# A two-layer encoder on one core: splits, gates and near-head transposes put in another order

## The chip, the cores and the metric

The kernel runs on one core of a Trainium2 chip. A core has a matrix engine (TensorE, PE in the profile, with its weight loads shown apart as PEld), VectorE (DVE), ScalarE (ACT), GpSimd (POOL) and a queue for transfers (SP). Each engine takes its own instructions strictly in the order written for it, and waits on semaphores for the others. The metric is device time in microseconds, from the first to the last instruction with a small fixed part around it; lower is better.

## The reference, cut to what matters

Two transformer layers over 1024 tokens of width 1024, with 256 memory tokens. Everything is float32.

```python
for l in range(2):
    h = rmsnorm(x, norm_gain[l])
    mk, mv = split(memn @ w_mem_kv[l])
    if l == 0:
        qa, ka, va, qb, kb, vb, qm, gate = split_cols(h @ w_in_even)
        ya = global_gqa(rope(rms(qa)), rope(rms(ka)), va)      # 8 heads of 64
        yb = window_gqa(qb, kb, vb, sink, rel_bias)            # 8 heads, +-128 tokens
        ym = memory_attn(qm, mk, mv)                           # 4 heads of 128
        y = concat(ya, yb, ym) * silu(gate)
    else:
        qc, kc, vc, qm, gate = split_cols(h @ w_in_odd)
        yc = neighborhood_attn(qc, kc, vc, rpb)                # 16 heads, 8 x 16 window
        ym = memory_attn(qm, mk, mv)
        y = concat(yc, ym) * silu(gate)
    x = x + y @ w_out[l]                                       # y: 1536 wide
return rmsnorm(x, final_gain)
```

## The kernel before

Every number is carried as a high and a low part, so that each product of matrices is three matmuls: high by high, high by low, low by high. A *split* is a copy to the high part on ACT (`copy`) and a subtraction for the low part on VectorE (L126 to L128). Weights are split the same way as they arrive (`w_parts`, L1263: `wraw` is the loaded tile, `wh` the copy on ACT, `wl` the subtraction on VectorE or GpSimd by turns).

The stages, in the order of time: the first projections (to about 143 us), the global and memory heads of layer 0, its window heads (about 500 to 671), output projection 0 (to about 778), the front of layer 1 (its projections, to about 1024), the memory heads of layer 1, its near heads (`near`, about 1130 to 1377), and output projection 1 with the final norm.

**The output projection** (`out_project`, L1297) uses a fast scheme of seven products in place of eight, on sums and differences of quarters of y and w. y is 12 rows of 128; each finished row k is multiplied by its gate and stored to memory as five half-width pieces, where rows 6 to 11 also need differences with row k - 6. The seven operands are called y11, t1, t2, t3, y22, y21 and t4. `y_parts` (L1209) loads the six pieces of one operand and splits them; of t1 and t2 the last three pieces are split later, inside the product (`later`). Each product is 72 matmuls of 512 columns, and PE takes them in the order a11 (with y11), s1 (t1), s2 (t2), s3 (t3), s4 (y22), a12 (y21), a22 (t4). The buffers of y22 are those of y11, and those of y21 are t1's.

**The near heads** run a loop over 128 blocks (16 heads of 8 blocks, L1149). In step n it transposes the probabilities of block n - 4 (`flips`, three transposes or two into a `tr` bank, then `p_parts`: copy `ph` on ACT, subtraction `pl` on VectorE), computes the scores of block n (`scores`: two matmuls; then on VectorE the bias addition with the row minimum, on ACT the exponential, on VectorE the reciprocal, on GpSimd the scaling of `pn`), multiplies block n - 5 by v (`values`), and lets PE do 1930 columns of other work (`fill`: k projections, gates, the first output product). PE keeps the order of the program here; the other engines do not.

**Gates.** `gated_steps` (L469) multiplies a finished row by its gate in two halves on VectorE, then makes the differences on GpSimd and the stores and loads on SP; it is a generator, one step of which is taken in each call of `scores` while `jobs` (splits of k weights) has nothing to do, or by `later_job` (L1935) in the last window heads. `gated` (L500) does the same in one go. `gate(k, tag)` (L1954) loads a gate of layer 1 from memory.

**Who sets the order.** Apart from PE in layer 1, a planner orders each engine's instructions: by priority (the order of the program, moved by the offsets in `AHEAD`) among those which its own simulation of time holds ready. `tc.issue_after(i)` ties what is written inside it: those instructions of the block that are on the engine of i are queued behind i. Instructions on other engines are not held by it. `behind_held` (L1202) ties to the last copy and the last low part of the near or window heads.

Of the kernel before, what the change touches and what calls it, by code (L numbers as in the profile page):

```python
# [64 lines left out]
class Trunk:  # L65
# [403 lines left out]
    def gated_steps(self, sg, y, yd, k):  # L469

        nc = self.nc
        first, second = slice(0, 512), slice(512, T)
        dst = yd[k]
        two = lambda t: t.rearrange("p (a n) -> p a n", a=2)
        nc.vector.tensor_tensor(y[:, second], y[:, second], sg[:, second], op=OP.mult)
        yield
        nc.vector.tensor_tensor(y[:, first], y[:, first], sg[:, first], op=OP.mult)
# [595 lines left out]
    def near(self, made, load_q, load_v, gate, yd, fill):  # L1073
# [12 lines left out]
        def scores(n):  # L1086
# [122 lines left out]
    def y_parts(self, yd, tags, kind, after=None):  # L1209
# [3 lines left out]
        for k, t in enumerate(self.halves(tags, F32R)):  # L1213
# [3 lines left out]
            with self.ahead("y"):  # L1217
# [8 lines left out]
                else:  # L1226
                    with self.behind_held(), self.tc.issue_after(after.ins) if after else nullcontext():
# [69 lines left out]
    def out_project(self, w, sd, yd, res, done, tags, banks, first, begun, last=False):  # L1297
# [26 lines left out]
        def products(y, banks, kind, start, ready=()):  # L1324
            ready = deque(ready)
            y, later = y
            ends.clear()
            for u in range(2):
                for i, bank in enumerate(banks):
                    (h, l), = (ready.popleft(),) if ready else weights(i, kind, (u,))  # L1330
                    for k in range(3):
                        for e, (s, m) in enumerate(((h, 0), (h, 1), (l, 0))):
                            end = nc.tensor.matmul(bank, s[:, k, :], y[3 * u + k][m], start=start and u + k + e == 0,
                                                   stop=u == 1 and k + e == 4, skip_group_check=True)
                    ends[u, i] = end
# [9 lines left out]
        def plus(x, p, op=OP.add):  # L1345
            nc.vector.tensor_tensor(x, x, p, op=op)
# [9 lines left out]
        ends = {}  # L1356
# [27 lines left out]
        y = self.y_parts(yd, tags["y"][3], "t3", after[0])  # L1384
        for i in range(4):
            end = product(y, xb[i], weights(i, "s3"), False)
# [6 lines left out]
        y = self.y_parts(yd, tags["y"][4], "y22", ends[1, 3])  # L1393
        for i in range(4):
            ending = product(y, yb[i], weights(i, "s4"), False)
# [7 lines left out]
        y = self.y_parts(yd, tags["y"][5], "y21", end)  # L1403
# [15 lines left out]
        y = self.y_parts(yd, tags["y"][6], "t4", ending)  # L1419
# [515 lines left out]
    def later_job(self, normal):  # L1935

        if self.later_jobs:
            with self.tc.issue_after(normal.ins):
# [3 lines left out]
    def odd(self, w, kvd, yd, vd, mqd, qd, gd):  # L1942
# [119 lines left out]
        for n in range(8):  # L2062
            h, g = divmod(n, 2)
            if g == 0:
                y = self.st("yb", [128, T])
                if h < 3:
# [10 lines left out]
            if g:  # L2077
                self.gated_rows(gate(8 + h), 8 + h, y, yd)
# [107 lines left out]
```

## Time and profile before

| | us |
|---|---|
| median of 3 runs | 1505.27 (1504.47 to 1507.01) |
| the profiled execution | 1505.1 |
| its span, first to last instruction | 1503.3 |
| TensorE busy | 1473.3 |
| VectorE busy | 1032.9 |
| ScalarE busy | 841.2 |
| GpSimd busy | 636.2 |

A row of a timeline gives the start in us, the duration in us, the engine, the line, the operation, the tiles written and read, how many instructions were merged into the row, and in brackets the idle time of the engine before it with what ended it. "SPq" is the issue of a transfer. A row of the wait lists gives who waited for whom, the total in us, the number of times and the longest. Matmuls overlap one another, so the distance between starts, not the duration, is what one costs.

### The profile page before, as it was taken

Reading aid. Unit: us, or ns where it says so; the run is one execution under the profiler, and the core shown is the slowest. Engines: PE = TensorE matmul, PEld = TensorE weight load, DVE = VectorE, ACT = ScalarE, POOL = GpSimd, SP = SyncE. Lnnn points to the kernel's source line nnn. Section 1 sums busy time; section 2 is a strip of 40 time slices with the busy share of each in tenths; the row PEclk is TensorE's granted clock in tenths of the full one; section 3 lists DMA queues with packets and bytes.
Section 4 is the critical chain, followed back from the end, with each engine's and each line's share of the span. In section 5 each row is a group of like instructions: output and inputs, shape, how many; then the busy total and the mean of one; then the engine's idle time right before and its main releaser. Section 6 shows DMA issues by size and latency. Waiting matters only on the chain.

```text
span 1503.3 us, 25289 instructions
## 1 busy us (share of the span) xinstructions
PE 1473.3 (98%) x8377; PEld 1266.8 (84%) x8377; DVE 1032.9 (69%) x2122; ACT 841.2 (56%) x1855; POOL 636.2 (42%) x762
## 2 busy tenths in 40 slices
PE   9999999999999999998999999999999999999997
PEld 8898888989888788786879877888988888888786
DVE  6786777677676677667577766654447778788744
ACT  7743665655655456554445444444447777777442
POOL 1223668556665655533450000002225556754355
PEclk9999999999999999999999999999999999999999
DMA  8966344433444423388653434558675677688833
GB/s 282 323 157 178 111 121 165 126 125 118 129 126 136 133 89 129 120 272 268 197 174 117 139 135 148 151 157 284 200 262 154 209 231 223 218 285 312 284 111 138
DMA packets 173859, 271.90 MB, mean 181 GB/s; under 512 B 15648, under 2 KB 96800, under 8 KB 172704
## 3 DMA queue, kind: packets, MB, share of 16 engines
q1 hardware_dynamic: 173296, 270.20, 56.0%
q8 instruction: 66, 1.08, 0.3%
q14 instruction: 65, 0.53, 0.1%
q10 hardware_dynamic: 432, 0.09, 0.0%
HBM read 174.28 MB, written 83.89 MB: 172 GB/s over the span
## 4 chain that ended last, share of the span: by engine, by line
PE 78%; DVE 7%; DMA 7%; issue 3%; ACT 2%; POOL 1%; SPq 1%; POOLq 0%; DVEq 0%; ACTq 0%
PE pj L241 15%; PE pj L62 10%; PE x L1585 6%; PE tr L132 5%; PE pv L1055 4%; PE y L1585 4%; PE pv L62 3%; PE pj L1319 3%; PE s L62 3%; PE sa L1319 2%; PE pv L1585 2%; PE tr L62 2%; PE s L1319 2%; PE sa L1022 2%; PE sa L1023 2%
## 5 line engine op out<-in xcount | busy, mean ns | idle before, releaser
L124 ACT ACTIVATE ph<-tr 128x512 fp32r<-128x512 f32 (+2 forms) x336 | 180.9, 540 | 118.3 <-PE tr L132 76.9
L537 DVE TENSOR_TENSOR pl<-tr,ph 128x512 fp32r<-128x512 f32 (+2 forms) x336 | 205.5, 615 | 54.0 <-ACT ph L124 52.9
L241 PE MATMUL pj<-H,wh 128*128 128x512 f32 x704 | 234.6, 413 | 0.5 <-DVE vt L312 0.2
L157 POOL TENSOR_SCALAR wh<-wraw 128x512 fp32r<-128x512 f32 x48 | 34.4, 719 | 268.3 <-PE x L1585 234.9
L124 ACT ACTIVATE wh<-wraw 128x384 fp32r<-128x384 f32 (+1 forms) x163 | 89.1, 553 | 89.9 <-PE pj L1319 12.0
L241 PE MATMUL pj<-H,wl 128*128 128x512 f32 x352 | 139.1, 395 | 0.0
L241 PEld LDWEIGHTS pj<-H,wh 128*128 128x128 f32 x704 | 120.0, 189 | 18.7 <-POOL wh L157 0.6
L62 PE MATMUL pj<-H,wh 128*128 128x512 f32 x384 | 121.5, 397 | 0.0
L1108 POOL TENSOR_SCALAR pn<-pn,st 128x384 f32<-128x384 f32 (+1 forms) x128 | 75.3, 589 | 99.6 <-DVE st L1107 58.0
L132 PE MATMUL tr<-ident,P 128*128 128x128 f32 x752 | 115.7, 273 | 0.9 <-DVE pl L537 0.6
L1267 POOL TENSOR_TENSOR wl<-wraw,wh 128x384 fp32r<-128x384 f32 x56 | 61.9, 1107 | 117.8 <-ACT wh L124 101.1
L132 PEld LDWEIGHTS tr<-ident,P 128*128 128x128 f32 x752 | 88.9, 140 | 9.6 <-DVE pl L537 1.7
L1028 ACT ACTIVATE P<-sa,st 128x1024 f32<-128x1024 f32 x64 | 71.5, 1118 | 41.5 <-DVE st L1027 22.7
L1106 ACT ACTIVATE pn<-pn,st 128x384 f32<-128x384 f32 (+1 forms) x128 | 75.1, 587 | 35.0 <-DVE st L1103 32.6
L62 PE MATMUL s<-k,q 128*128 128x384 f32 (+1 forms) x352 | 86.5, 342 | 0.1
L1030 POOL TENSOR_SCALAR P<-P,st 128x1024 f32<-128x1024 f32 x64 | 73.9, 1158 | 29.0 <-DVE st L1029 26.9
L1027 DVE TENSOR_REDUCE st<-sa 128x1 f32<-128x1024 f32 x64 | 77.6, 1218 | 10.9 <-PE sa L1023 10.5
L241 PEld LDWEIGHTS pj<-H,wl 128*128 128x128 f32 x352 | 66.2, 188 | 15.1
L62 PE MATMUL pj<-H,wl 128*128 128x512 f32 x192 | 75.8, 395 | 0.0
L159 POOL TENSOR_TENSOR wl<-wraw,wh 128x512 fp32r<-128x512 f32 x52 | 68.2, 1315 | 9.5 <-ACT wh L124 6.9
L62 PEld LDWEIGHTS pj<-H,wh 128*128 128x128 f32 x384 | 66.6, 189 | 5.5
L840 PE MATMUL pj<-ah,H 128*128 128x256 f32 x384 | 70.5, 282 | 0.2
(558 smaller groups left out, 4172.3 us busy)
## 6 DMA issues: line engine op xcount, KB each, us to landing
wraw<-w_o SPq DMA_DIRECT2D x52, 256.0 KB, 3.7
y<-yb SPq DMA_DIRECT2D x24, 512.0 KB, 3.6
wraw<-s SPq DMA_DIRECT2D x64, 192.0 KB, 3.4
wraw<-w_e SPq DMA_DIRECT2D x44, 256.0 KB, 3.2
k<-k SPq DMA_DIRECT2D x42, 256.0 KB, 4.8
s<-bias SPq DMA_DIRECT2D x56, 192.0 KB, 2.0
y<-sg SPq DMA_DIRECT2D x20, 512.0 KB, 3.6
wq<-w_o SPq DMA_DIRECT2D x40, 256.0 KB, 3.3
```

The source lines that it names most:

```text
L62: return lambda *a, **k: self.tc.keep_in_program_order(getattr(self.engine, name)(*a, **k))
L124: return self.nc.scalar.activation(out, in_, AF.Copy, scale=scale)
L132: self.turned = self.fence = self.pe.transpose(o, i, self.ident)
L241: self.pe.matmul(a[:, :n], s[:, kt % UNIT, :], m, start=(kt == 0 and i == 0), stop=(kt == KT - 1 and i == 2))
L537: self.low = nc.vector.tensor_tensor(pl[:, :n], tr[:, :n], ph[:, :n], op=OP.subtract)
L1027: nc.vector.tensor_reduce(st[:, 0:1], s, axis=AX.X, op=OP.max, negate=True)
L1028: nc.scalar.activation(pt, s, AF.Exp, bias=st[:, 0:1], accum_out=st[:, 1:2])
L1030: self.normal = nc.gpsimd.tensor_scalar(pt, pt, st[:, 2:3], 0.5, op0=OP.mult, op1=OP.mult)
L1106: nc.scalar.activation(o, o, AF.Exp, bias=st[:, 0:1], scale=-1.0, accum_out=st[:, 2:3])
L1108: normal = nc.gpsimd.tensor_scalar(o, o, st[:, 3:4], 0.5, op0=OP.mult, op1=OP.mult)
L1319: last = nc.tensor.matmul(bank, s[:, k, :], y[3 * u + k][m][:, cols], start=start and u + k + e == 0, stop=u == 1 and k + e == 4, skip_gro ...
L1585: self.last = nc.tensor.matmul(bank, ws[s][:, k, :], b[k][m], start=start and k + i == 0, stop=k == UNIT - 1 and i == 2, skip_group_check= ...
```

## The change

- `y_parts` and `products`: the tie of the splits of t3, y22, y21 and t4 is no longer to a matmul but to two instructions: the last weight copy (`self.high`, ACT) and the last addition of a product (`self.added`, VectorE) written at that point. The later splits of t1 and t2 are tied to the last weight copy too.
- `near`: transposes are made for two blocks, n - 5 and n - 4, in each even step; the multiplication by v is of block n - 6 in place of n - 5, and the loop has one step more.
- `gated_steps`: each multiplication and the differences of rows below 6 come after `gap` empty steps (1 in the window heads, 2 in the near heads), and its instructions on VectorE are tied to the last low part (`self.low`) as well as, on GpSimd, to the last scaling.
- The memory heads of layer 1 load their gate when a head begins and not when it ends, into two buffers by turns (`sg` and `mk`), and the fourth head's gate is done in steps during the near heads.

```diff
-    def gated_steps(self, sg, y, yd, k):
+    def gated_steps(self, sg, y, yd, k, gap=1):
...
+        for _ in range(gap):
+            yield
         nc.vector.tensor_tensor(y[:, second], y[:, second], sg[:, second], op=OP.mult)
-        yield
+        for _ in range(gap):
+            yield
         nc.vector.tensor_tensor(y[:, first], y[:, first], sg[:, first], op=OP.mult)
         if k < 6:
-            yield
+            for _ in range(gap):
+                yield
...
-                with self.tc.issue_after(normal.ins):
+                with self.tc.issue_after(normal.ins), self.tc.issue_after(self.low.ins):
                     while jobs and next(jobs[0], self) is self:
...
-        for n in range(128 + 5):
-            if 4 <= n < 132:
-                parts[n - 4] = flips(n - 4)
-                if n == 131:
+        for n in range(128 + 6):
+            for f in (n - 5, n - 4) if n % 2 == 0 else ():
+                if 0 <= f < 128:
+                    parts[f] = flips(f)
+                if f == 127:
                     self.held = self.copies[-1], self.low
...
-            if n >= 5:
-                values(n - 5)
-                if (n - 5) % 16 == 15:
-                    j = (n - 5) // 16
-                    self.later_jobs.append(self.gated_steps(pair[j]["g"], pair[j]["y"], yd, ROWS.index(j)))
+            if n >= 6:
+                values(n - 6)
+                if (n - 6) % 16 == 15:
+                    j = (n - 6) // 16
+                    self.later_jobs.append(self.gated_steps(pair[j]["g"], pair[j]["y"], yd, ROWS.index(j), 2))
...
-    def behind_held(self):
+    def behind_held(self, more=()):
         with ExitStack() as held:
-            for i in self.held:
+            for i in (*self.held, *more):
...
-                    with self.behind_held(), self.tc.issue_after(after.ins) if after else nullcontext():
+                    with self.behind_held(after):
                         self.split(hi, lo, raw)
...
-        self.copy(hf, raw)
+        self.high = self.copy(hf, raw)
...
                     elif later:
-                        with self.behind_held(), self.ahead("y"):
+                        with self.behind_held((self.high,)), self.ahead("y"):
                             self.split(*later.popleft())
...
-            nc.vector.tensor_tensor(x, x, p, op=op)
+            self.added = nc.vector.tensor_tensor(x, x, p, op=op)
...
+            if i == 1:
+                after = self.high, self.added
-        after = [ends[1, 0]]
...
-        y = self.y_parts(yd, tags["y"][3], "t3", after[0])
+        y = self.y_parts(yd, tags["y"][3], "t3", after)
+        after = self.high, self.added
...
-        y = self.y_parts(yd, tags["y"][4], "y22", ends[1, 3])
+        y = self.y_parts(yd, tags["y"][4], "y22", after)
+        after = self.high, self.added
...
-        y = self.y_parts(yd, tags["y"][5], "y21", end)
+        y = self.y_parts(yd, tags["y"][5], "y21", after)
+        after = self.high, self.added
...
-        y = self.y_parts(yd, tags["y"][6], "t4", ending)
+        y = self.y_parts(yd, tags["y"][6], "t4", after)
...
             if g == 0:
                 y = self.st("yb", [128, T])
+                sg = gate(8 + h, ("sg", "mk")[h % 2])
...
-            if g:
-                self.gated_rows(gate(8 + h), 8 + h, y, yd)
+            if g and h < 3:
+                self.gated_rows(sg, 8 + h, y, yd)
+            elif g:
+                self.later_jobs.append(self.gated_steps(sg, y, yd, ROWS.index(11), 2))
```

More of the change, by code (lines that the diff above doesn't have):

```diff
@@ L1201, in behind_held, with y_parts @@
     @contextmanager
-    def behind_held(self):
+    def behind_held(self, more=()):
         with ExitStack() as held:
-            for i in self.held:
+            for i in (*self.held, *more):
                 held.enter_context(self.tc.issue_after(i.ins))
             yield
-    def y_parts(self, yd, tags, kind, after=None):
+    def y_parts(self, yd, tags, kind, after=()):
         nc = self.nc
@@ L1326, in products @@
             y, later = y
-            ends.clear()
             for u in range(2):
@@ L1332, in products @@
                         for e, (s, m) in enumerate(((h, 0), (h, 1), (l, 0))):
-                            end = nc.tensor.matmul(bank, s[:, k, :], y[3 * u + k][m], start=start and u + k + e == 0,
-                                                   stop=u == 1 and k + e == 4, skip_group_check=True)
-                    ends[u, i] = end
+                            nc.tensor.matmul(bank, s[:, k, :], y[3 * u + k][m], start=start and u + k + e == 0,
+                                             stop=u == 1 and k + e == 4, skip_group_check=True)
                     if u:
@@ L1383, in out_project @@
         sums = []
-        y = self.y_parts(yd, tags["y"][3], "t3", after[0])
+        y = self.y_parts(yd, tags["y"][3], "t3", after)
+        after = self.high, self.added
         for i in range(4):
-            end = product(y, xb[i], weights(i, "s3"), False)
+            product(y, xb[i], weights(i, "s3"), False)
             residual(at(c21, i), 4 + i, 1)
@@ L1391, in out_project @@
                 square(at(c22, i), i)
-        y = self.y_parts(yd, tags["y"][4], "y22", ends[1, 3])
+        y = self.y_parts(yd, tags["y"][4], "y22", after)
+        after = self.high, self.added
         for i in range(4):
-            ending = product(y, yb[i], weights(i, "s4"), False)
+            product(y, yb[i], weights(i, "s4"), False)
             with self.ahead("sink"):
@@ L1937, in later_job @@
         if self.later_jobs:
-            with self.tc.issue_after(normal.ins):
+            with self.tc.issue_after(normal.ins), self.tc.issue_after(self.low.ins):
                 if next(self.later_jobs[0], self) is self:
```

1 line of the change is left out of this document (removed).

## The prediction, made before the result was known

> **What bounds the kernel now.** I read the page first, then the table of stages, then the list of who waited for whom on TensorE, and last the timelines of the few places where TensorE waits.
>
> ```profile
> span 1503.3 us, 25289 instructions
> PE 1473.3 (98%) x8377; PEld 1266.8 (84%) x8377; DVE 1032.9 (69%) x2122; ACT 841.2 (56%) x1855; POOL 636.2 (42%) x762
> ```
> ```profile
> 671.00:706.00 35.00, 31.05 (x129) 23.59 (x128) 23.73 (x34) 16.47 (x32) 11.91 (x10) 1.00 0.89 302
> 1128.00:1137.00 9.00, 7.97 (x39) 5.96 (x38) 6.34 (x19) 5.78 (x15) 5.50 (x7) 1.00 0.50 167
> 1137.00:1377.00 240.00, 236.87 (x1384) 204.25 (x1383) 188.62 (x581) 176.46 (x448) 136.83 (x188) 1.00 0.73 236
> 1402.00:1423.00 21.00, 18.86 (x80) 14.72 (x79) 15.18 (x20) 11.75 (x22) 8.59 (x7) 1.00 0.89 315
> ```
> TensorE (PE) is busy for 98% of the span, at a granted clock of 1.00 in all these stretches, so nothing but removed matmuls or removed waits of PE can shorten the run. The change removes no matmul. What can be won is idle time: 4.0 us of 35 in the first output projection (671 to 706), 1.0 of 9 where the near heads begin (1128), 3.1 of 240 in the near heads, 2.1 of 21 in the second output projection (1402). (Columns: the stretch, its length, then busy time and instructions of PE, its weight loads, VectorE, ScalarE and GpSimd, granted clock, DMA share, GB/s.) Who ended PE's waits, over the whole run (total, times, longest):
>
> ```profile
> PE pv L62 <- DVE pl L537: 2.7, 7, 0.8
> PE pj L1333 <- DVE wl L1267: 2.4, 1, 2.4
> PE pj L1319 <- DVE wl L1267: 1.9, 1, 1.9
> PE tr L1333 <- DVE wl L1267: 1.0, 1, 1.0
> PE tr L62 <- POOL pn L1108: 0.9, 2, 0.7
> PE sa L692 <- DVE st L696: 0.9, 2, 0.5
> PE pj L1333 <- ACT wh L124: 0.4, 1, 0.4
> PE pj L1319 <- ACT wh L124: 0.2, 1, 0.2
> ```
> Each of the eight lies in a stage that the change touches; together they are 10.4 us. A wait costs more than its listed idle time, as one of the seven waits for a low part shows (PE, then VectorE):
>
> ```profile
> 1168.62 0.49 PE L62 MATMUL tr<-ident,pn 128*128 128x128 f32 x3
> 1168.86 0.60 PE L62 MATMUL s<-k,q 128*128 128x384 f32 x2
> 1169.30 0.34 PE L62 MATMUL pv<-ph,v 128*128 128x384 f32 x1
> 1169.91 0.44 PE L62 MATMUL pv<-pl,v 128*128 128x384 f32 x1 [0.28 <-DVE pl L537]
> 1170.19 0.62 PE L62 MATMUL pj<-H,wh 128*128 128x512 f32 x2
> 1171.63 0.34 PE L62 MATMUL pv<-pl,v 128*128 128x384 f32 x1
> 1154.20 0.34 PE L62 MATMUL pv<-ph,v 128*128 128x384 f32 x1
> 1154.55 0.63 PE L62 MATMUL pj<-H,wh 128*128 128x512 f32 x2
> ```
> ```profile
> 1168.72 0.67 DVE L475 TENSOR_TENSOR yb<-yb,sg 128x512 f32<-128x512 f32 x1
> 1169.31 0.55 DVE L537 TENSOR_TENSOR pl<-tr,ph 128x384 fp32r<-128x384 f32 x1
> 1193.68 0.91 DVE L477 TENSOR_TENSOR yb<-yb,mk 128x512 f32<-128x512 f32 x1
> ```
> By starts, the two steps from 1169.30 to 1170.19 take 0.89 us; undisturbed (1154.20 to 1154.55) they take 0.35. So 0.54 is lost where 0.28 is listed: 0.26 more for each wait, which I add below.
>
> **The change, part by part.**
>
> *Splits of y tied to ACT and DVE (both output projections).* A tie only orders instructions of the tying instruction's own engine. The old tie of a later product's splits named a matmul, and a split is a copy on ScalarE (ACT) and a subtraction on VectorE (DVE): it held nothing. The trace agrees (two rows of y splits on ACT, and between them bt):
>
> ```profile
> 674.92 0.63 ACT L124 ACTIVATE q<-q 128x512 fp32r<-128x512 f32 x1 [4.15 <-DMA q<-y]
> 675.58 0.60 ACT L124 ACTIVATE bt<-pv 64x512 f32<-64x512 f32 x1
> 686.04 0.63 ACT L124 ACTIVATE va<-va 128x512 fp32r<-128x512 f32 x1 [5.08 <-DMA va<-y]
> ```
> At 674.92 ACT takes a part of y22, which is first multiplied two products later, and sits 4.15 us before it for the load; again 5.08 us before 686.04. Queued behind it are the copies of the weights that PE wants now (wh), and also bt, the last window block, on which the gate of row 7 hangs. With the tie to the last weight copy and the last addition of the product before, these splits come some 16 us later, when their loads have long landed. What goes: 1.0 + 0.4 + 2.4 us and 3 x 0.26, 4.6 at most. What is late next: the loads, whose engines are at 0.89 here and which are not moved, so that the parts of t1 that land last still set some wait. Nothing to 4.6; I take 3.6, near the upper end, because the wait is for the order and not for the bytes PE needs.
>
> The moved splits (6 copies and 6 subtractions to a product, of 0.63 and about 0.68 us) now lie beside the product ahead of their own. They are 4.1 us of DVE in about 17 us of PE (72 matmuls; 129 take 31.05 us in the stretch from 671), next to some 8 additions and 4 weight subtractions: it fits, but any that slips shows as a wait for wl. I charge 1.0 (0 to 3).
>
> In the second output projection the same splits delay the last gate:
>
> ```profile
> 1382.63 0.59 ACT L124 ACTIVATE bt<-pv 64x512 f32<-64x512 f32 x1
> 1392.09 1.50 DVE L475 TENSOR_TENSOR yb<-yb,mk 128x512 f32<-128x512 f32 x1
> 1409.06 4.14 SPq L1223 DMA_DIRECT2D H<-y  x6
> 1415.68 3.88 ACT L124 ACTIVATE H<-H 128x512 fp32r<-128x512 f32 x6
> ```
> The order is bt, the gate's multiplication, the row's stores, the load of t2's last part, and behind it in SP's queue the six loads of t3 (1409.06), whose copies (1415.68) stand ahead of the weights for which PE waits 1.9 and 0.2 us in the list (L1319). With y22's and y21's splits gone from the front, bt and the gate come some 5 us earlier and the chain with them. 1.9 + 0.2 + 2 x 0.26 = 2.6 at most; I take 2.0, since the DMA share is 0.89 here as well.
>
> *Gates tied to low parts, with gaps.* In the near loop one gate multiplication or the gate's split stands directly ahead of the pl that PE waits for in all six waits inside the loop (1168.72 and 1193.68 are two); the seventh is at the end of the loop. Tied behind the low part just traced, and with two calls between the steps, a multiplication comes right after both low parts of a pair, and two iterations pass before the next. 2.7 x 6/7 + 6 x 0.26 = 3.9, and I take it all: what covers the 0.67 to 0.91 us of the multiplication is two iterations, some 3.7 us (240 us for 129 of them); behind it in VectorE's queue stands a bias addition whose block is transposed three iterations later. Where that cover is gone, each of the 14 costs what it costs today. The longer gate chain (10 calls for 7) ends, with its stores and its load on SP and its three GpSimd subtractions, some 5 us later; its buffers are wanted again two pairs later, 30 us. In the window heads the same tie moves a multiplication of that size from before the bias additions (0.9 listed, 1.4 with restarts): 0.6, between 0 and 1.4.
>
> *Transposes of two blocks in one run.* It saves no PE time of its own: three transposes take 0.24 us (1168.62 to 1168.86), and the two 384-wide matmuls after them 0.44 in place of 2 x 0.175, so 0.33, 0.11 each; eight in one run take the same:
>
> ```profile
> 152.28 1.03 PE L132 MATMUL tr<-ident,P 128*128 128x128 f32 x8
> 153.07 0.71 PE L241 MATMUL pj<-H,wh 128*128 128x512 f32 x2
> 153.61 0.39 PE L241 MATMUL pj<-H,wl 128*128 128x512 f32 x1
> ```
> (0.79, and 0.54 after it in place of 2 x 0.24: 0.85, 0.11 each.) What it gives is time: the second block of a pair is used two iterations after its transposes and no longer one, the first still after one. The instructions of VectorE and ACT that meet there, in the near stage:
>
> ```profile
> L1103 DVE CUSTOM_DVE_ANT_0 pn<-s,bm 128x384 f32<-128x384 f32 x92 | 50.8, 552 | 19.1 <-PE s L62 9.6 <-PE pv L62 3.2 <-POOL pn L1108 2.4
> L360 DVE TENSOR_TENSOR k<-pj,k 64x512 fp32r<-64x512 f32 x26 | 17.8, 686 | 1.8 <-ACT k L124 1.4
> L124 ACT ACTIVATE ph<-tr 128x384 fp32r<-128x384 f32 x96 | 46.9, 489 | 18.4 <-PE tr L62 16.7 <-PE s L62 0.3
> ```
> The 26 k evictions that can sit ahead of a low part then hurt half as often: 0.5 (0 to 1.5; their waits are too short to be listed). At the loop's end the last block's parts are used right after their transposes, with no filler left: a copy and a subtraction (0.49 and 0.55) less the matmuls between, so +0.5 lost (0 to 1.0).
>
> *Two gate buffers; the fourth memory gate as later steps.*
>
> ```profile
> 1129.44 1.23 DVE L509 TENSOR_TENSOR yb<-yb,sg 128x1024 f32<-128x1024 f32 x1 [3.19 <-DMA sg<-g]
> ```
> The multiplication holds DVE for 3.19 us for its gate's load, the first near blocks' bias additions wait behind it, and PE finds its first pn late (0.9 listed, in two waits). With the load a head earlier and this gate in steps, 0.9 + 2 x 0.15 goes; I take 1.1. The other three memory gates win nothing, as none of PE's listed waits is theirs; on SP the four loads only go ahead of k's copies by some 0.5 us of issue each.
>
> One contention speaks against it all:
>
> ```profile
> L475 DVE TENSOR_TENSOR yb<-yb,mk x4: 891/914/1501, 1199.8 to 1392.1; 128x512 f32<-128x512 f32 x4
> ```
> The multiplication that took 0.67 us at 1168.72 takes up to 1.50 here: something holds it. The Trainium skill (SBUF — State Buffer, "SBUF: two separate sides") says that a VectorE instruction with two SBUF inputs and a GpSimd one that reads SBUF exclude each other for a whole instruction; by that rule the trace agrees, and the moved splits, which have two SBUF inputs, would meet GpSimd's weight subtractions anew. By the rows alone I keep the 1.0 charged above; with the rule taken hard the sum would be that of the second rival.
>
> **Sum.** 3.6 + 2.0 + 3.9 + 0.6 + 0.5 + 1.1 = 11.7 won, 1.0 + 0.5 = 1.5 lost, 10.2 net: 1505.1 us of the profiled execution (span 1503.3 and 1.8 around it) gives 1494.9. The median shown, 1505.27, is 0.2 above it, so 1495. All upper ends and no charge give 4.6 + 2.6 + 3.9 + 1.4 + 1.5 + 1.2 = 15.2, 1490.
>
> **The rivals.** First, *the loads end last.* For it: a DMA share of 0.89 in both output stretches, and loads that keep their order. Against it: ACT's 4.15 and 5.08 us are for parts wanted much later. Then the output projections give a third, 1.9 in place of 5.6: 1498.6, and with the upper charges (3 and 1.0) 1501.1.
>
> Second, *splits and weight subtractions hold each other.* A held one takes 1.50 for 0.68, 0.82 more. Of the 24 splits of y22 and y21 in two layers, one in five reaching PE costs 5 x (0.82 + 0.26) = 5.4: 1500.3.
>
> Third, *the change does not do what it says*: the planner, which orders by its own estimate of time, puts other early work in the places freed, and the waits only change names. Then only the 1.1 of the fourth memory gate is left, 1504.
>
> Fourth, the other side: *pairs make the first block late.* From the end of its transposes (1168.95) to its low part's use at 1171.63 are 2.68 us, 2.1 without the 0.54 lost between; copy and subtraction take 0.49 and 0.55, hand-overs some 0.3, so 0.8 is spare. One VectorE operation of 0.68 ahead of pl fits; in a pair the second block's copy and subtraction and a bias addition of 0.55 come into the same stretch, and if a second one goes ahead, PE waits about 0.4 + 0.26. From 16 of 64 pairs on (16 x 0.66 = 10.6) the gain is gone; at every second pair, 32 x 0.66 = 21, it is 1516. Against it: 20% of DVE's time is free there, and the spare time of the first block is what it is today.
>
> **How the numbers follow.** A measurement of this kernel tells 0.2% (3 us) from no change. Forecast (1490 to 1499): 0.48. First and second rival (1499 to 1502): 0.22. Third, between 1502.3 and 1508.3: 0.12. Fourth, or a new order that costs as much: 0.18. Faster 0.70, same 0.12, slower 0.18. The range leaves out a tenth at each side: 1489 to 1508.
>
> **What would show it.** Right: ACT's idle time ended by y loads between 671 and 706 falls from the 9.2 of the two rows shown to under 4; no L475, L477 or L483 directly ahead of a late pl; "pv L62 <- pl L537" under 0.7 us; "wl L1267" gone as PE's releaser at 1333 and 1319; L509 not at the start of the near heads. Wrong: that list with as many waits under other names; pv waiting for ph or pl in every second iteration; PE waiting for wraw's loads.

## The result

The changed kernel is faster: 1496.78 us (1495.29 to 1499.33) against 1504.87 us for the kernel before beside it, 8.1 us less. The ratio on record is 0.9925 with a 95% interval of 0.9906 to 0.9944, which is 11.3 us; the two medians alone give 0.9946. Beside the experiments the kernel before had medians of 1507.26 to 1508.97 us, and against these 1496.78 is 0.992 to 0.993. So the gain lies between 8 and 11 us. The forecast was 1495, in a range of 1489 to 1508.

The page of the changed kernel:

```profile
span 1497.5 us, 25309 instructions
PE 1471.1 (98%) x8377; PEld 1271.2 (85%) x8377; DVE 1036.7 (69%) x2123; ACT 833.8 (56%) x1855; POOL 635.1 (42%) x762
```

The same work, and only 5.8 us less span in the two profiled executions. What is missing lies ahead of the change: up to the window heads every engine has the same instructions in the same order, and yet that part took 501.5 us before and 505.3 after. So below, whole kernels are compared by their ratios, and places by the lengths of stages, from the first matmul of a stage to the first or last one that bounds it:

| stage, us | before | changed | difference |
|---|---|---|---|
| window heads and output projection 0 | 277.53 | 272.23 | -5.30 |
| front and memory heads of layer 1 | 354.97 | 354.94 | -0.03 |
| near heads | 243.11 | 242.13 | -0.98 |
| output projection 1 | 119.19 | 116.07 | -3.12 |

How far one profile can be trusted shows in kernels that have the same order of instructions as the kernel before in a stage. In the first row two of them (the pairs alone and the gate buffers alone, below) take 278.82 and 279.40 us, so about 2 us stay open there; in the near heads two others (the splits' ties alone, all or four of them) take 243.36 and 243.66 for the 243.11 of before. In output projection 1 the four kernels with the old ties take 118.40 to 120.37 us and the ten with the new ones 115.89 to 117.30.

The gain is in the two output projections. The first of them has no idle matrix engine left; the near heads have more idle time than before, 4.8 us of 242.1 where it was 4.1 of 243.1. Busy time by stretches (the columns of the prediction's table of stages): the two output projections of the changed kernel, its near heads, and the near heads of the kernel before:

```profile
675.00:710.00 35.00, 35.00 (x152) 28.21 (x151) 21.61 (x30) 17.09 (x34) 14.40 (x12) 1.00 0.90 313
1400.00:1421.00 21.00, 21.00 (x92) 16.96 (x91) 14.17 (x20) 11.99 (x24) 5.92 (x5) 1.00 0.91 313
1132.50:1374.60 242.10, 237.28 (x1395) 209.26 (x1393) 189.77 (x588) 173.93 (x453) 136.24 (x191) 1.00 0.76 238
```
```profile
1134.00:1377.10 243.10, 239.03 (x1395) 205.75 (x1393) 190.53 (x590) 178.40 (x454) 139.52 (x191) 1.00 0.73 237
```

Who ended TensorE's waits in the near heads (1125 to 1390) of the changed kernel:

```profile
PE pv L62 <- DVE pl L541: 2.9, 6, 0.8
PE tr L62 <- POOL pn L1112: 1.8, 2, 1.1
```

The wait for low parts (pl), 2.7 us in 7 before, is 2.9 in 6. It was to fall under 0.7. And there are two long waits for normalised blocks (pn) late in the loop; the two of before, 0.9 us together, lay at its start.

**What these waits are.** No gate multiplication stands directly ahead of a late low part any more; other work does. The longest case (TensorE, then the main rows of VectorE, then GpSimd):

```profile
1295.64 0.45 PE L62 MATMUL pv<-ph,v 128*128 128x384 f32 x1
1296.92 0.44 PE L62 MATMUL pv<-pl,v 128*128 128x384 f32 x1 [0.84 <-DVE pl L541]
```
```profile
1291.43 1.74 DVE L477 TENSOR_TENSOR yb<-yb,sg 128x512 f32<-128x512 f32 x1
1293.17 0.53 DVE L1107 CUSTOM_DVE_ANT_0 pn<-s,bm 128x384 f32<-128x384 f32 x1
1293.64 0.68 DVE L360 TENSOR_TENSOR k<-pj,k 64x512 fp32r<-64x512 f32 x1
1294.49 0.17 DVE L1111 RECIPROCAL st<-st 128x1 f32<-128x1 f32 x1 [0.17 <-ACT pn L1110]
1295.11 0.69 DVE L360 TENSOR_TENSOR k<-pj,k 64x512 fp32r<-64x512 f32 x1 [0.45 <-ACT k L124]
1295.83 0.56 DVE L1107 CUSTOM_DVE_ANT_0 pn<-s,bm 128x384 f32<-128x384 f32 x1
1296.31 1.02 DVE L541 TENSOR_TENSOR pl<-tr,ph 128x384 fp32r<-128x384 f32 x2
```
```profile
1291.35 1.28 POOL L501 TENSOR_TENSOR yb<-mk,yb 128x512 f32<-128x512 f32 x1
```

The tied multiplication does stand behind a pair of low parts (the two L541 that end at 1291.5). But it began 0.08 us after a GpSimd subtraction and took 1.74 us instead of 0.68. VectorE is then late for the whole next pair, whose first block's low part stands behind two k evictions and a bias addition; TensorE loses 1.1 us: its two starts lie 1.28 us apart, undisturbed 0.18. The Trainium skill (SBUF — State Buffer, "SBUF: two separate sides") says that such a pair of instructions excludes each other for a whole instruction; the trace agrees here in the main (VectorE's ends 0.54 us after GpSimd's, a little less than the 0.68 that it takes alone). In this profile the 13 multiplications of L477 and L480 that share no time with a GpSimd instruction take 0.67 to 0.68 us, the 7 that do 0.68 to 1.74.

The two late normalised blocks (GpSimd, then TensorE):

```profile
1342.85 1.28 POOL L498 TENSOR_TENSOR mk<-yb,mk 128x512 f32<-128x512 f32 x1
1344.11 0.59 POOL L1112 TENSOR_SCALAR pn<-pn,st 128x384 f32<-128x384 f32 x1
1370.11 1.27 POOL L498 TENSOR_TENSOR sg<-yb,sg 128x512 f32<-128x512 f32 x1
1371.35 0.48 POOL L1112 TENSOR_SCALAR pn<-pn,st 128x256 f32<-128x256 f32 x1
```
```profile
1344.76 0.33 PE L62 MATMUL tr<-ident,pn 128*128 128x128 f32 x1 [0.68 <-POOL pn L1112]
1371.89 0.33 PE L62 MATMUL tr<-ident,pn 128*128 128x128 f32 x1 [1.15 <-POOL pn L1112]
```

The scaling of a block waits behind one of the gate's three subtractions, 1.3 us long. The pairs need both blocks' pn at once.

Last, the stores. The last store of a near row begins at 1314.05 before and at 1326.59 in the changed kernel; the closing addition that needs its buffer comes at 1330.16 and 1329.91 (GpSimd's subtraction, store and addition of before, then an earlier addition, the store and the addition of the changed kernel):

```profile
1312.73 1.29 POOL L497 TENSOR_TENSOR yb<-sg,yb 128x512 f32<-128x512 f32 x1
1314.05 0.32 SPq L498 DMA_DIRECT2D y<-yb  x1
1330.16 0.67 DVE L1147 TENSOR_TENSOR yb<-pv,bt 64x512 f32<-64x512 f32 x1
```
```profile
1297.80 0.68 DVE L1151 TENSOR_TENSOR yb<-pv,bt 64x512 f32<-64x512 f32 x1 [0.47 <-DMA y<-yb]
1326.59 0.33 SPq L502 DMA_DIRECT2D y<-yb  x1
1329.91 0.67 DVE L1151 TENSOR_TENSOR yb<-pv,bt 64x512 f32<-64x512 f32 x1
```

The gate chain ends 12.5 us later, and 16 us of room have become 3. Here the store lands in 2.3 us, before the addition; at 1297.80 another closing addition does wait 0.47 us for such a store.

### The profile page after: what moved, and what is told of

Its sections match the earlier page's. It is cut to its first block, busy times and chain, and to the rows that moved or that the text cites. A ratio compares the mean times of both kernels' runs of the same rounds, so it can differ in the third digit from the quotient of the medians.

```text
span 1497.5 us, 25309 instructions
## 1 busy us (share of the span) xinstructions
PE 1471.1 (98%) x8377; PEld 1271.2 (85%) x8377; DVE 1036.7 (69%) x2123; ACT 833.8 (56%) x1855; POOL 635.1 (42%) x762
## 5 line engine op out<-in xcount | busy, mean ns | idle before, releaser
L541 DVE TENSOR_TENSOR pl<-tr,ph 128x512 fp32r<-128x512 f32 (+2 forms) x336 | 202.9, 615 | 66.9 <-ACT ph L124 65.6
L124 ACT ACTIVATE ph<-tr 128x512 fp32r<-128x512 f32 (+2 forms) x336 | 174.8, 539 | 114.6 <-PE tr L132 82.4
L1112 POOL TENSOR_SCALAR pn<-pn,st 128x384 f32<-128x384 f32 (+1 forms) x128 | 71.8, 562 | 109.4 <-DVE st L1111 67.8
L62 PE MATMUL s<-k,q 128*128 128x384 f32 (+1 forms) x352 | 81.4, 327 | 0.0
```

Source lines behind the costliest of these rows:

```text
L62: return lambda *a, **k: self.tc.keep_in_program_order(getattr(self.engine, name)(*a, **k))
L124: return self.nc.scalar.activation(out, in_, AF.Copy, scale=scale)
L541: self.low = nc.vector.tensor_tensor(pl[:, :n], tr[:, :n], ph[:, :n], op=OP.subtract)
L1112: normal = nc.gpsimd.tensor_scalar(o, o, st[:, 3:4], 0.5, op0=OP.mult, op1=OP.mult)
```

## The experiments

**The four parts alone.** Each is one part of the diff shown above, put into the kernel before. Microseconds worked out of a ratio are shares of 1504.87.

*The splits' ties alone.*

```diff
-        self.copy(hf, raw)
+        self.high = self.copy(hf, raw)
-        y = self.y_parts(yd, tags["y"][4], "y22", ends[1, 3])
+        y = self.y_parts(yd, tags["y"][4], "y22", after)
+        after = self.high, self.added
```
(and likewise t3, y21, t4, and the later splits of t1 and t2)

> The kernel before with the ties of the splits of y alone. Theory: the two output projections lose their waits for wl because the early splits leave ACT's queue; output projection 0 from 108.3 to about 103 us, output projection 1 from 119.2 to about 116, near stage unchanged at 243, the whole run 8 us faster (about 1497). Rival: the two stages gained because the gates before them ended earlier; then this run wins under 3 us and PE still waits for wl there.

Measured: 0.9944 (0.9927 to 0.9960), 8.4 us. Window heads and output projection 0 take 273.34 us, output projection 1 takes 115.89, the near heads 243.36. This is three quarters of the gain of the whole change by the ratios, and 7.5 of 9.4 us by the stages. It is not free: one weight copy (wh) now stands on ScalarE behind seven copies of parts of y, and TensorE waits for it:

```profile
706.89 0.73 PE L1319 MATMUL pj<-H,wh 128*128 128x512 f32 x2 [0.97 <-ACT wh L124]
```

*The pairs alone.*

```diff
-        for n in range(128 + 5):
-            if 4 <= n < 132:
-                parts[n - 4] = flips(n - 4)
+        for n in range(128 + 6):
+            for f in (n - 5, n - 4) if n % 2 == 0 else ():
+                if 0 <= f < 128:
+                    parts[f] = flips(f)
```

> The kernel before with transposes in pairs alone (and the multiplication by v one step later). Theory: the near stage loses the short waits behind k evictions for every second block, but keeps gate multiplications ahead of pl: 0 to 2 us faster. Rival (first block of a pair late): a wait of pv for pl in many pairs, near stage 3 to 15 us longer.

Measured: 0.9992 (0.9978 to 1.0007); near heads 242.91. By themselves the pairs do nothing that can be told.

*The gates' tie and gaps alone.*

```diff
-                with self.tc.issue_after(normal.ins):
+                with self.tc.issue_after(normal.ins), self.tc.issue_after(self.low.ins):
-    self.later_jobs.append(self.gated_steps(pair[j]["g"], pair[j]["y"], yd, ROWS.index(j)))
+    self.later_jobs.append(self.gated_steps(pair[j]["g"], pair[j]["y"], yd, ROWS.index(j), 2))
```

> The kernel before with gate steps tied to the last low part and gaps between them, alone. Theory: the six waits for pl behind a gate multiplication go, near stage 4 us shorter (239), the window heads 0.6. Rival: without pairs the tied multiplication stands ahead of the next step's pl, and the waits stay: 0 to 1 us.

Measured: 1.0046 (1.0029 to 1.0063), 6.9 us slower where 4 us less was expected. The near heads take 248.60, 5.5 more. Window heads and output projection 0 take 279.28; that is 1.75 more, but no more than the two kernels with the old order there (278.82 and 279.40), so no loss is shown. TensorE's longest waits in this kernel, and where the one of the window heads comes from (ScalarE, then TensorE):

```profile
PE pv L737 <- ACT ph L124: 3.1, 1, 3.1
PE s L62 <- DMA k<-k: 2.9, 2, 1.5
```
```profile
666.92 0.63 ACT L124 ACTIVATE H<-H 128x512 fp32r<-128x512 f32 x1 [6.87 <-DMA H<-y]
667.99 0.60 ACT L124 ACTIVATE ph<-tr 128x512 fp32r<-128x512 f32 x1
668.63 0.38 PE L737 MATMUL pv<-ph,v 128*128 128x256 f32 x1 [3.15 <-ACT ph L124]
```

In the window heads ScalarE sits 6.87 us before a split of y (H) with the probabilities (ph) queued behind it: with the gate later, y's stores and loads are later (the store of the row's differences starts at 659.22, before at 644.46), and the untied splits make everything behind them wait. So the gates' tie alone moves the waiting that the splits' ties cure into the window heads; output projection 0, from the last window matmul on, is shorter in turn, 103.71 for 108.30. In the near heads a closing addition holds VectorE for 1.17 us, the k evictions behind it come late, and TensorE waits for the transfer of k twice, the first time until 1344.66 (a store, VectorE, TensorE). The profile names GpSimd as the addition's releaser; the store that frees its buffer, 5.9 us from issue to landing, ended just then as well, at 1336.0, and which of them it was stays open:

```profile
1330.12 0.32 SPq L502 DMA_DIRECT2D y<-yb  x1
1336.13 0.68 DVE L1151 TENSOR_TENSOR yb<-pv,bt 64x512 f32<-64x512 f32 x1 [1.17 <-POOL wl L1271]
1336.74 0.67 DVE L360 TENSOR_TENSOR k<-pj,k 64x512 fp32r<-64x512 f32 x1
1344.66 0.36 PE L62 MATMUL s<-k,q 128*128 128x256 f32 x1 [1.42 <-DMA k<-k]
```

Close behind both of these long waits the granted clock falls to half:

```profile
670.50:673.90 3.40, 3.22 (x8) 2.57 (x9) 0.37 (x2) 0.00 (x0) 0.00 (x0) 0.50 0.88 262
1346.30:1349.70 3.40, 3.22 (x12) 2.82 (x13) 1.15 (x4) 0.60 (x2) 1.07 (x2) 0.50 1.01 328
```

At half clock 3.4 us hold the work of 1.7, so about 1.7 of the 5.5 us of the near heads are clock (an estimate from these rows). The mean granted clock of this kernel's eight runs is 0.9934, that of the 25 runs of the kernel before beside them 0.9965; the difference, 0.0031 of 1510 us, is some 4.7 of the 6.9 us (an estimate too). What brings such a fall on stays open. Of the profiles here the kernels with the pairs alone (at 692.7), without the pairs (1341.9) and with the buffer of its own (1332.6) have one in these stages, each next to a wait of TensorE of 1.4 us or more; but the wait of 2.38 us at 692.7 in the kernel before has none. The other profiles have no fall in these stages.

*The gate buffers and the fourth memory gate alone.*

```diff
+                sg = gate(8 + h, ("sg", "mk")[h % 2])
-            if g:
-                self.gated_rows(gate(8 + h), 8 + h, y, yd)
+            if g and h < 3:
+                self.gated_rows(sg, 8 + h, y, yd)
+            elif g:
+                self.later_jobs.append(self.gated_steps(sg, y, yd, ROWS.index(11)))
```

> The kernel before with the memory gates loaded a head earlier into two buffers, and the fourth gate in steps, alone. Theory: VectorE's 3.19 us wait for the gate's load goes and PE's first pn is there in time: about 1 us faster. Rival: pn of the first blocks stays late for another reason, no change.

Measured: 0.9998 (0.9984 to 1.0012); the near heads take 241.74, 1.4 less, as their first pn is no longer late. Too little for the ratio to tell, visible in its stage, where kernels of one order differ by about 0.6.

The four ratios added give 3.0 us faster; the whole change gives 11.3. The parts are not independent.

**One part left out of the changed kernel.**

*Without the pairs.*

```diff
-        for n in range(128 + 6):
-            for f in (n - 5, n - 4) if n % 2 == 0 else ():
-                if 0 <= f < 128:
-                    parts[f] = flips(f)
+        for n in range(128 + 5):
+            if 4 <= n < 132:
+                parts[n - 4] = flips(n - 4)
```

> The changed kernel without the pairs: splits tied, gates tied with two-call gaps, two gate buffers, but one block transposed per iteration as before. Alone, the gate tie made the near heads 5.5 us longer (243.1 to 248.6) and the whole 7 us slower; with the pairs the near heads are 1.0 us shorter. Theory A, the pairs are what makes the tie affordable: near heads 246 to 249, out projections as in the changed kernel (103 and 116), total about 1502 against 1508 before, ratio 0.995 to 0.998. Rival B, the tie's loss alone came from the window heads and the old places of the splits of y, and the pairs matter little: near heads 241 to 243, ratio 0.991 to 0.993.

Measured: 0.9957 (0.9942 to 0.9971); near heads 247.35, window heads and output projection 0 272.50, output projection 1 116.17. Theory A: without pairs the tie costs 5.6 us in the near heads (241.74 to 247.35), with them next to nothing. Of the 5.6 about 1.7 are again a fall of the clock, behind two waits for k:

```profile
1341.90:1345.30 3.40, 3.40 (x15) 3.00 (x13) 1.23 (x5) 1.09 (x3) 1.71 (x2) 0.51 1.03 307
```

The 3.15 us wait of the window heads is gone; here the splits are tied.

*Without the near and window tie and its gaps.*

```diff
-                with self.tc.issue_after(normal.ins), self.tc.issue_after(self.low.ins):
+                with self.tc.issue_after(normal.ins):
```
(in both loops, and one call between the steps)

> The changed kernel with the gate multiplications untied and with one call between them, as before. Theory A, with pairs the tie is worth what the trace of the changed kernel shows, about 1 us in the near heads and 1 us at the window heads: near heads 243, window heads and output projection 0 together 273.5 (272.2 in the changed kernel, 273.4 with the splits alone), ratio 0.994 to 0.995. Rival B, the tie costs also with pairs, as it did alone: near heads 240 to 241 and a ratio of 0.990 to 0.991, better than the changed kernel.

Measured: 0.9926 (0.9905 to 0.9947), as good as the changed kernel (0.9925). Near heads 241.41; window heads and output projection 0 273.73. Neither theory quite: the near heads are not worse without the tie, the window heads are 1.5 us worse, a little more than the 1 us of theory A.

*Of the splits' ties, only those of t3, y22, y21 and t4*, in the kernel before:

```diff
-                        with self.behind_held((self.high,)), self.ahead("y"):
+                        with self.behind_held(), self.ahead("y"):
                             self.split(*later.popleft())
```
(against the splits' ties alone)

> Of the splits' ties only those of the products t3, y22, y21 and t4 (their splits behind the last weight copy and addition of the product before); the later splits of t1 and t2 stay as before. Theory A, the old tie to a matmul held nothing on ScalarE and VectorE, and this is the whole gain: output projection 0 at 104.7 (108.3 before), output projection 1 at 116 (119.2), ratio 0.994 to 0.995. Rival B, the later splits of t1 and t2, which had no tie either, are what stood ahead of the weights: output projections at 106 to 108 and 117.5 to 119, ratio 0.997 to 0.999.

Measured: 0.9930 (0.9909 to 0.9952); output projection 0 104.36 (104.70 with all of the splits' ties), output projection 1 116.22. The old tie to a matmul was the whole fault; the later splits of t1 and t2 add nothing that can be told.

**What holds the near heads.**

*One call between the steps, the tie kept.*

```diff
-    self.later_jobs.append(self.gated_steps(pair[j]["g"], pair[j]["y"], yd, ROWS.index(j), 2))
+    self.later_jobs.append(self.gated_steps(pair[j]["g"], pair[j]["y"], yd, ROWS.index(j)))
```
(and for the fourth memory gate)

> The changed kernel with one call between a gate's steps again; the tie stays. With two calls the last store of a near gate starts at 1326.6, where it started at 1314.1 before, and a later closing addition waits for it (0.97 us lost at 1329.9). Theory A, the longer gate chain is part of what was given back: near heads 240.5 to 241.5, ratio 0.991 to 0.992. Rival B, the gaps keep the multiplications off the low parts, and without them two meet in one pair: near heads 243 to 245, ratio 0.993 to 0.995.

Measured: 0.9909 (0.9884 to 0.9933), but near heads 242.29, as in the changed kernel: neither theory. The losses at 1296.9, 1344 and 1371 are gone. One of 2.24 us has come, behind a store that took 9.2 us to land (store, addition and TensorE), and 1.9 us behind k transfers. (The expectation put the 0.97 us at 1329.9 down to the store; as said above, that one had landed, and the addition only stood ahead of the low parts.)

```profile
1314.74 0.40 SPq L502 DMA_DIRECT2D y<-yb  x1
1324.03 0.68 DVE L1151 TENSOR_TENSOR yb<-pv,bt 64x512 f32<-64x512 f32 x1 [2.47 <-DMA y<-yb]
1326.24 0.39 PE L62 MATMUL pv<-pl,v 128*128 128x256 f32 x1 [2.08 <-DVE pl L541]
```

*The same, with the last difference in a buffer of its own.*

```diff
-        nc.gpsimd.tensor_tensor(y[:, second], sg[:, second], y[:, second], op=OP.subtract)
-        nc.sync.dma_start(dst[:, 4, :], y[:, second])
+        d = self.st("vt", [128, 512]) if own else y[:, second]
+        nc.gpsimd.tensor_tensor(d, sg[:, second], y[:, second], op=OP.subtract)
+        nc.sync.dma_start(dst[:, 4, :], d)
```

> The kernel with one call between a gate's steps, and the last difference of a near gate written to a buffer of its own, so that the buffer of y is free when the difference is read and not when its store has landed (the store took 9.2 us there, and PE lost 2.24 us at 1323.9 behind the closing addition that waited for it). Theory A, the store's landing is the wait: this loss goes and near heads take 239.5 to 240.5 (242.3 before this edit). Rival B, the closing addition then waits for the subtraction itself or the store of the row's first part: near heads 241.5 or more.

Measured: 0.9902 (0.9883 to 0.9922), near heads 242.63. The 2.24 us went, as theory A has it, but the stage is no shorter. TensorE's waits in its near heads, and the stretch behind the second wait for k:

```profile
PE s L62 <- DMA k<-k: 2.3, 2, 1.4
PE pv L62 <- DVE pl L542: 1.1, 3, 0.5
```
```profile
1332.60:1336.00 3.40, 3.07 (x9) 2.78 (x10) 1.44 (x5) 0.60 (x2) 1.28 (x3) 0.50 1.02 289
```

The k transfers, behind which 1.9 us were lost with the stall, now cost 1.13 and 1.60 us at 1330 and 1331, and the clock falls right there, about 1.7 us more. Without that fall the stage would be at 240.9 (an estimate), near the range of theory A; the ratio does not tell this kernel from the one with the shared buffer (0.9909).

*The tie at the window heads alone* (near heads untied, one call).

```diff
-                with self.tc.issue_after(normal.ins), self.tc.issue_after(self.low.ins):
+                with self.tc.issue_after(normal.ins):
                     while jobs and next(jobs[0], self) is self:
```

> The changed kernel with the tie of the gate multiplications kept at the window heads alone; the near heads' multiplications are untied, with one call between steps. From the runs so far: window heads and output projection 0 take 272.2 to 272.5 us in every kernel with the window tie and the splits' ties, 273.3 to 273.7 without the window tie; the near heads 241.4 without the tie and 242.1 with it. Theory A, the two ties act separately: 272.3 and 241.4, output projection 1 at 116.0, so 0.8 us less than the changed kernel, ratio 0.990 to 0.993. Rival B, the near heads' tie is also worth something that the one profile of the untied kernel did not show: near heads 242.5 or more, ratio 0.993 to 0.995.

Measured: 0.9917 (0.9898 to 0.9937); 271.28 and 242.05. The ties act separately. With the same order in the near heads, on all four engines, as the kernel without either tie (241.41), the stage differs by 0.6: so much a stage varies from one execution to another, and the near tie is worth nothing that these profiles can tell, between 0.7 lost and 0.1 lost.

*Without GpSimd's three subtractions.* Left out is the making of the differences for the rows of the window and near heads; the stores carry other values.

```diff
-        nc.gpsimd.tensor_tensor(sg[:, second], y[:, first], sg[:, second], op=OP.subtract)
         yield
-        nc.gpsimd.tensor_tensor(sg[:, first], y[:, first], sg[:, first], op=OP.subtract)
         nc.sync.dma_start(dst[:, 2:4, :], two(sg))
         yield
-        nc.gpsimd.tensor_tensor(y[:, second], sg[:, second], y[:, second], op=OP.subtract)
         nc.sync.dma_start(dst[:, 4, :], y[:, second])
```

> The changed kernel without GpSimd's three subtractions of the later rows' gates (window and near heads); the stores stay and carry other values, so this part of the computation is left out. Theory A, these subtractions, which the longer chain pushes together, cause the late normalised blocks (0.84 and 1.31 us lost at 1343.8 and 1370.5), the held multiplication ahead of 1296.9 (1.1) and part of the late store (0.97): near heads 238 to 239.5. Rival B, GpSimd is not at fault, the bias additions and evictions on VectorE are, and other work comes late in the same places: near heads 241 to 242.5.

Measured: 0.9882 (0.9861 to 0.9903); near heads 237.87, 4.3 less. Its waits for low parts, and its near stage in the columns used above (GpSimd's 117.60 us are the last busy time):

```profile
PE pv L62 <- DVE pl L538: 1.0, 4, 0.5
1125.50:1363.30 237.80, 236.48 (x1394) 209.33 (x1392) 187.84 (x588) 173.38 (x453) 117.60 (x176) 1.00 0.76 243
```

Theory A: 15 subtractions of 1.29 us, none of which TensorE needs there, cost 4.3 us through what stands behind them. The stores start earlier without them too; how much of the 4.3 is theirs, this run doesn't tell. What is left is 1.6 us of first blocks of pairs behind a k eviction or an addition of that size, and 1.1 at the loop's end.

*The same subtractions on VectorE*, in the near heads.

```diff
-        nc.gpsimd.tensor_tensor(sg[:, second], y[:, first], sg[:, second], op=OP.subtract)
+        engine = nc.vector if gap == 2 else nc.gpsimd
+        engine.tensor_tensor(sg[:, second], y[:, first], sg[:, second], op=OP.subtract)
```
(and the other two)

> The changed kernel with the near gates' three subtractions on VectorE in place of GpSimd (15 of 1.29 us become 15 of about 0.68). Left out altogether, they gave back 4.3 us of near heads (242.1 to 237.9). Theory A, what costs is their place on GpSimd, where the scaling of the normalised blocks waits behind them and VectorE's multiplications are held: near heads 238.5 to 240.5, ratio 0.988 to 0.991. Rival B, on VectorE they stand ahead of low parts instead (a subtraction of 0.68 stands directly ahead of one in three places of its order): near heads 241 to 243, ratio 0.991 to 0.994.

Measured: 0.9933 (0.9916 to 0.9950), near heads 243.65, a little above the range of theory B. The three waits of its near heads, and a row of VectorE:

```profile
PE pv L62 <- DVE pl L542: 2.6, 6, 0.8
PE tr L62 <- DVE pl L542: 1.4, 1, 1.4
PE tr L62 <- POOL pn L1113: 0.6, 2, 0.3
```
```profile
1340.46 0.69 DVE L497 TENSOR_TENSOR mk<-yb,mk 128x512 f32<-128x512 f32 x1 [2.63 <-DMA mk<-y]
```

Late pn on GpSimd falls from 1.8 to 0.6 and late pl rises from 2.9 to 4.0. Each subtraction is half as long there (0.68 us), but VectorE is the engine that already makes TensorE wait. TensorE's longest wait, 1.4 us, is not for a subtraction's length: VectorE sits 2.63 us before one for the load of its other operand (mk), and a low part stands behind it.

No version is shown to beat the changed kernel. Of the two best, 0.9909 lies inside its interval and 0.9902 just below it, and the interval of 0.9902 (up to 0.9922) overlaps it.

## Why the prediction was right, and where it was not

The total was right: 10.2 us forecast, 8.1 by the medians and 11.3 by the ratio measured, 9.6 in the two profiles from the window heads to the end. It was right by luck, as two errors cancel. For the window heads and the output projections together the steps gave 3.6 + 2.0 + 0.6 - 1.0 = 5.2, and 8.4 came; for the near heads they gave 3.9 + 0.5 + 1.1 - 0.5 = 5.0, and 1.0 came.

- **The splits' old tie held nothing.** Right, and shown by undoing it alone. In the changed kernel ScalarE's idle time before y22's parts (q and va), 4.15 and 5.08 us, is gone between 674 and 709 us; what is left is for parts of the products at hand (H, v). All idle time ended by loads of y falls from 16.9 us (671 to 706) to 7.8, not under 4 as the prediction's sign had it:

```profile
L124 ACT ACTIVATE H<-H 128x512 fp32r<-128x512 f32 x9 | 5.5, 622 | 5.0 <-DMA H<-y 4.9
L124 ACT ACTIVATE v<-v 128x512 fp32r<-128x512 f32 x2 | 1.3, 632 | 2.9 <-DMA v<-y 2.9
L124 ACT ACTIVATE q<-q 128x512 fp32r<-128x512 f32 x2 | 1.1, 616 | 0.0
L124 ACT ACTIVATE va<-va 128x512 fp32r<-128x512 f32 x2 | 1.1, 614 | 0.0
```

- **Output projection 0, 3.6.** 3.6 in the kernel with these ties alone (108.30 to 104.70).
- **Output projection 1, 2.0, at most 2.6.** Too small: 3.3 alone, 3.1 in the changed kernel. The sum left out a third wait of this stage, of 0.33 us in this row of before, which with its restart cost 0.6, and it took 2.0 of the 2.6 because of a DMA share of 0.89, which held nothing back (it is 0.91 in the changed kernel):

```profile
1387.49 0.50 PE L1333 MATMUL tr<-k,wl 128*128 128x512 f32 x1 [0.33 <-POOL wl L1267]
```

- **The moved splits, 1.0 lost.** Nothing in the changed kernel: TensorE waits for no wl and no wh in either of its output projections. But the term was not empty: TensorE waits 0.97 us for a wh with the splits' ties alone, and 0.52 us at the same place with the subtractions on VectorE. In the changed kernel the same run of copies stands ahead of that wh, from 703.37 to 707.01, and TensorE just does not wait. That the loads end last (first rival), or that splits and weight subtractions hold each other (second), did not happen there.
- **The window heads' gate, 0.6, 0 to 1.4.** 1.4: 272.2 us on average over the six whole kernels with this tie and the splits' ties (271.3 to 272.5), 273.6 over the three without it (273.3 to 273.7). Alone it brings the wait of 3.15 us above, which the step did not foresee: the tie delays y's loads, and only tied splits do not mind.
- **Near gates tied to low parts, 3.9, "and I take it all".** This is the step that failed; 0.1 to 0.7 lost came instead. The multiplications did leave the low parts. But the step's cover, "its buffers are wanted again two pairs later, 30 us", was wrong: the chain ends 12.5 us later and not 5, and the room was 16 us from the store's start, less its landing. And it counted only the multiplications. The chain's GpSimd subtractions hold VectorE's multiplications and stand ahead of pn; 4.3 us hang on them.
- **The pairs, 0.5 won and 0.5 lost.** Alone, 0.2 won. What was not seen: they carry the tie, which costs 5.6 us without them, some 1.7 of it clock. The fourth rival's mechanism is there at the first blocks with a k eviction ahead, 0.3 to 0.65 us each and four times in the kernel without the subtractions, far from the 16 pairs at which it would have decided. The spare time was 0.6 us and not 0.8, as the transposes end at 1169.11 and not at 1168.95, so one k eviction of 0.68 does not quite fit.
- **The fourth memory gate, 1.1.** 1.4 alone.
- **The third rival**, other work in the places freed, holds for the near heads, where the waits changed names, and nowhere else.
- **That a wait costs 0.26 more than listed.** It does at the wait of this last row (0.6 for 0.33) and at 1296.9 (1.1 for 0.84).

## What to carry to other kernels

A tie that names an instruction of another engine holds nothing: look whether the tied instruction really comes late in the profile. Before taking one blocker away from a late instruction, list all that stand ahead of it in the same queue and what stands behind the moved one (here GpSimd's subtractions, a store, the k transfers), since the next one takes its place; the cost of a part depends on which others are there, so leave each one out of the whole as well as trying it alone. Before a stage's length is taken as the price of a part, look whether the granted clock fell in it and how much the stage varies where nothing was changed. And when a sum comes out right, compare it stage by stage before believing its steps.

## What the runs showed of the chip

A 256 KB store from the same line took 2.3 us to land in the changed kernel, 4.5 before, 5.9 and 9.2 in two others; why is not shown. A VectorE multiplication of 0.68 us took up to 1.74 next to a GpSimd subtraction. Ahead of the run's last few microseconds the granted clock fell to 0.50 for 3.4 us nine times in eight of the fourteen profiles, each time next to a wait of TensorE of 1.2 us or longer. And the part ahead of the window heads took from 500.1 to 505.3 us in profiles of kernels that differ only behind it.
